# Router work inside an output projection, another order of weight buffers, and a sum of experts in two parts

## The chip, the core and the metric

The kernel runs on one core of a Trainium2 chip. Its time is the device time of one execution in microseconds (us). The engines in the rows are PE (TensorE, matrix products and transposes), PEld (its weight loads), DVE (VectorE), ACT (ScalarE), POOL (GpSimd) and SP (SyncE, which here issues most of the DMA transfers). An engine's instructions run in the order of its own queue; between engines they wait on semaphores.

## The reference

Two transformer blocks run one after the other on 256 tokens of 1024 features, in float32. The change lies in the first: a hybrid mixer ends in an output projection `w_out`, and behind it comes a mixture of 32 experts.

```python
x = x + gate_m * hybrid_mixer(...)            # ends in: merged @ w_out
h = rmsnorm(x, norm_ffn) * (1.0 + scale_f) + shift_f
x = x + gate_f * hierarchical_moe(h, ...)

def hierarchical_moe(h, w_rg, b_rg, w_re, b_re, w_gate, w_up, w_down):
    g_logits = tok @ w_rg + b_rg              # 4 groups; one is chosen
    e_logits = tok @ w_re + b_re              # 8 experts a group; two are chosen
    ...
    for e in range(N_EXPERTS):
        hid = silu(tok @ w_gate[e]) * (tok @ w_up[e])
        out = out + combine[:, e:e + 1] * (hid @ w_down[e])
```

The three weights of an expert are 1 MB each.

## The kernel before

**Dense products.** The activations lie with features on the partitions: `xT[:, n]` is a slice of 128 features by 256 tokens, and there are eight of them. `dense_B` makes each slice of an output as a tile: for each of eight slices k of the input three products (`mm3`, L653 to L655), since weights and input are both split into a high and a low part. With `lead=True` the first three tiles run interleaved by k, in the order in which the input slices become ready (`gate_of`); the others follow one by one, 24 products each. When a tile is done, `evac` is called: for the output projection, "wout", that is `ev_wout`, which adds the tile to `xT` (L1183), scales it for the router into `xa` (L1184) and hands it to `Squares`, whose ScalarE squares serve the mean of squares of the next norm.

**Weights.** The class `Weights` issues all loads on SyncE in one fixed order, each as soon as its buffer is free; a load whose buffer isn't free holds up all behind it. For dense layers a loaded piece becomes a unit: ScalarE copies its high part (L211), VectorE subtracts for the low one (L212), into slots called `whl`.

**Experts.** There are 96 expert matrices (eight groups of four experts, each gate, up, down), loaded as jobs 0 to 95 into 16 buffers in turn: nine `rawb`, two "w" (the `whl` slots 2 and 3, each taken as two halves), five `rawa`. The "w" buffers are handed to the loader by `ws.pool("w", ...)` only when wout and its units are done, in the code just ahead of the expert rounds. There are four rounds r, each with `gate_up(r, 0)`, `down(r, 0)`, `gate_up(r, 1)`, `down(r, 1)`; each product of the first kind is L1407. A round's result is put into `xT` by `combine` within the next round, after its first `gate_up`; the last one, `combine(*before, True)`, stands behind all rounds and makes the squares and sums for the final norm on the way. In round 1 a branch (`If`) leads to a slower path that is not taken with these inputs.

**Router.** The token-major copy of `xa` (transposes, L1203) and the 36 logits (L1204) are made slice by slice after wout. The norm's root (`rsqrt`, 12 small VectorE operations) and the bias row `rbb` turn them into `lg` (L1208); then come the choice of group and experts (L1239 to L1267), the tables of slots, and the products that gather the tokens (L1366), which feed the first `gate_up`. `token_major` makes the token-major activations `ht` from the transposes with help of ScalarE and GpSimd (L1221, L1222, L1229). The constant vector `b1` of the norm's shift is spread over tokens (`brow`) and run through the router weights by `shift_rows` (L1164 on): a generator put into `pipes`, of which `dense_B` runs a step at given places, four products, four, and eight.

**PSUM** has eight banks. `psum_banks(n)` gives n to the tag "acc" (tiles of `dense_B`) and 7 − n to "mis"; during wout n is 3.

Of the kernel before, what the change touches and what calls it, by code (L numbers as in the profile page):

```python
# [19 lines left out]
T = 256  # L20
# [249 lines left out]
def _trace(ctx, tc, A, out, dbg, stop):  # L270
# [9 lines left out]

    def psum_banks(n, **kw):

        pscope.close()
        psums["acc"] = n, pscope.enter_context(tc.tile_pool(name=f"pacc{n}", bufs=n, space=PSUM, **kw))
        psums["mis"] = 7 - n, pscope.enter_context(tc.tile_pool(name=f"pm{n}", bufs=7 - n, space=PSUM, **kw))

# [6 lines left out]
    def mis():  # L293
        return acc("mis")
# [52 lines left out]
    for pr in range(8):  # L347
        for m in ("expert_w_gate", "expert_w_up", "expert_w_down"):
            for e in range(4 * pr, 4 * pr + 4):
                src = A[m][0, e]  # L350
                q = j % (NA + NB + NW)
                pool = "b" if q < NB else "w" if q < NB + NW else "a"
                j += 1
                at = [(o, 1024) for o in (0, 1024)] if pool == "w" else [(0, 2048)]
                ws.add((m, e), [(None, bass.AP(tensor=src.tensor, offset=src.offset + o, ap=[[2048, 128], [1, n]]))
                                for o, n in at], (2048,), pool=pool)
# [206 lines left out]
    def run(g):  # L563
        for _ in g:
            pass
# [582 lines left out]
    with ExitStack() as l1:  # L1148
# [9 lines left out]
        gate = mods[0][:, 40:48]  # L1158
        xa = wk.tile([128, 8, T], FT, name="xa", tag="X", bufs=2)
        brow = wk.tile([128, 1024], FT, name="brow", tag="X", bufs=2)  # L1160
# [17 lines left out]

        pipes.append(shift_rows())
        sq = Squares()  # L1180

        def ev_wout(n, ps, w):
            V.scalar_tensor_tensor(xT[:, n], ps[:, :T], mods[0][:, 16 + n:17 + n], xT[:, n], op0=OP.mult, op1=OP.add)  # L1183
            V.tensor_scalar(xa[:, n], xT[:, n], a1[:, n:n + 1], None, op0=OP.mult)  # L1184
            sq.add(xT[:, n])

        dense_B("wout", cols256(0, 1024), 1024, lambda k: ohi[:, k], lambda k: olo[:, k], ev_wout, lead=True,
# [5 lines left out]
        if stop == "x_mix0":  # L1193
            return
        psum_banks(4, reuse_waits="tile")
        tp = [[acc() for _ in range(2)] for _ in range(2)]
        lps = [mis() for _ in range(2)]
        for kt in range(8):
            if kt == 3:
                ps = mis()  # L1200
                sq.mean(ps)
            for c in range(2):
                P.transpose(tp[kt // 4][c][:, kt % 4 * 128:kt % 4 * 128 + 128], xa[:, kt, c * 128:(c + 1) * 128], ident)  # L1203
                P.matmul(lps[c][:, :36], xa[:, kt, c * 128:(c + 1) * 128], wr[:, kt], start=(kt == 0), stop=(kt == 7))  # L1204
        rm = rsqrt(ps[:, 0:2])
        lg = wk.tile([128, 2, 36], FT, name="lg")
        for c in range(2):
            V.scalar_tensor_tensor(lg[:, c], lps[c][:, :36], rm[:, c:c + 1], rbb, op0=OP.mult, op1=OP.add)  # L1208

        hth = hl.tile([128, 2, 8, 128], FR, name="hth", tag="h8", bufs=2)  # L1210
        htl = hl.tile([128, 2, 8, 128], FR, name="htl", tag="h8", bufs=2)

        ht = wk.tile([128, 4, 512], FT, name="ht", tag="X", bufs=2)

        def token_major(g, c, eng):
            t_ = ht[:, 2 * g + c]
            bg = brow[:, g * 512:(g + 1) * 512]
            if eng is V:
                V.scalar_tensor_tensor(t_, tp[g][c], rm[:, c:c + 1], bg, op0=OP.mult, op1=OP.add)
            else:  # L1220
                S.activation(t_, tp[g][c], AF.Copy, scale=rm[:, c:c + 1])  # L1221
                G.tensor_tensor(t_, t_, bg, op=OP.add)  # L1222
            pv = t_.rearrange("t (a q k) -> t a q k", a=4, q=16)
            oh = hth[:, c].rearrange("t k (a q) -> t a q k", q=16)[:, 4 * g:4 * g + 4]
            ol = htl[:, c].rearrange("t k (a q) -> t a q k", q=16)[:, 4 * g:4 * g + 4]
            yield True
            S.activation(oh, pv, AF.Copy)
            yield True
            eng.tensor_tensor(ol, pv, oh.bitcast(FT), op=OP.subtract)  # L1229
# [221 lines left out]

        def combine(Ys, C, last=False):

# [4 lines left out]
            for f in range(8):  # L1458
                ps = mis()
                for p_ in range(2):  # L1460
                    for i in range(2):
                        P.matmul(ps[:, :T], Ys[p_][i][:, f * 128:(f + 1) * 128], C[p_][0], start=(p_ + i == 0),
                                 stop=(p_ + i == 2))
                V.scalar_tensor_tensor(xT[:, f], ps[:, :T], gate[:, f:f + 1], xT[:, f], op0=OP.mult, op1=OP.add)
# [12 lines left out]

        ws.pool("w", ws.whl, 2, 3)
        ws.pump()
        ready, before = deque(), None  # L1480
# [4 lines left out]
        for r in range(4):  # L1485
# [13 lines left out]
            next(nxt, None)  # L1499
            Ys = [down(r, 0, hT, C[0][1])]  # L1500
            hid = gate_up(r, 1, X)
            next(nxt, None)
# [6 lines left out]
            before = Ys, C  # L1509
        sums = combine(*before, True)  # L1510
        if stop == "moe":
# [653 lines left out]
```

## Time and profile before

| what | us |
|---|---|
| three runs | 1554.55, 1557.94, 1560.27 (median 1557.94) |
| the profiled execution, its own time | 1556.02 |
| its span | 1554.2 |
| busy: PE, DVE, ACT, POOL | 1380.5, 898.1, 633.0, 359.2 |
| wout, from its first product | 263.18 to 290.87 |
| wait for the first product of the router's gather (L1366) | until 311.31 |
| expert rounds, first to last product | 317.42 to about 537 |

All times within the kernel are from the start of the span of the profiled execution. The rows further below have their start first, then their length. A product's length in the rows (0.28 us for a dense one) is more than its share of the engine, since products overlap; the pace is read from the starts.

### The profile page before, as it was taken

What the parts mean: (1) busy time and instruction counts of PE and PEld (TensorE: products, weight loads), DVE (VectorE), ACT (ScalarE), POOL (GpSimd) and SP (SyncE); (2) the same over time, 40 slices, a digit from 0 to 9 for tenths busy, and PEclk for the clock granted to TensorE, in tenths of its full rate; (3) what the DMA queues carried; (4) which work ended last, traced back from release to release, by engine and by line L of the source; (5) the groups of instructions that cost most, each with busy time, mean ns of one, the idle gap of its engine ahead of it and who ended that gap; (6) DMA issues with size and microseconds to landing.
All of it is one profiled execution on the core that took longest, in us unless ns stands there. A gap on an engine that the chain in (4) does not pass through costs nothing.

```text
span 1554.2 us, 29404 instructions
## 1 busy us (share of the span) xinstructions
PE 1380.5 (89%) x12145; PEld 1184.7 (76%) x12145; DVE 898.1 (58%) x1683; ACT 633.0 (41%) x1117; POOL 359.2 (23%) x402
## 2 busy tenths in 40 slices
PE   3978699796687689999998899999999998999997
PEld 1757578763343389888997786899998887899997
DVE  3676666631112287877664566665555787765544
ACT  2633223320101257544443454454443766554432
POOL 3163642100000011154256203900000574000000
PEclk9998789896978889999999899999999999999998
DMA  8883456979999985655799976776557564877540
GB/s 309 295 284 125 154 163 217 361 293 418 374 417 419 359 140 152 209 180 170 178 179 168 234 200 204 208 207 178 174 182 217 177 190 136 244 193 188 176 150 28
DMA packets 283613, 344.00 MB, mean 221 GB/s; under 512 B 18249, under 2 KB 258368, under 8 KB 265552
## 3 DMA queue, kind: packets, MB, share of 16 engines
q1 hardware_dynamic: 272016, 335.33, 67.9%
q0 software_dynamic: 10848, 5.33, 3.5%
q8 instruction: 97, 1.59, 0.4%
q10 hardware_dynamic: 608, 1.39, 0.2%
q14 instruction: 44, 0.36, 0.1%
HBM read 340.63 MB, written 1.10 MB: 220 GB/s over the span
## 4 chain that ended last, share of the span: by engine, by line
PE 51%; DMA 9%; DVE 7%; ACT 3%; POOL 2%; issue 2%; POOLq 0%; SPq 0%; DVEq 0%; ACTq 0%
PE acc L653 14%; PE acc L654 14%; PE acc L655 14%; DMA rawa<-in_hy_w_in_dram 3%; DMA rawb<-in_expert_w_up_dram 3%; DVE wlo L212 2%; PE adaps L524 2%; POOL c L2029 1%; PE acc L1407 1%; DMA rawb<-in_expert_w_gate_dram 1%; PE mis L1740 1%; DMA rawa<-in_expert_w_up_dram 1%; DMA rawa<-in_expert_w_gate_dram 1%; ACT whi L211 1%; DVE q L1695 1%
## 5 line engine op out<-in xcount | busy, mean ns | idle before, releaser
L212 DVE TENSOR_TENSOR wlo<-rawa,whi 128x1024 fp32r<-128x1024 f32 (+1 forms) x303 | 378.2, 1252 | 252.2 <-ACT whi L211 251.4
L653 PE MATMUL acc<-hhi,whi 128*128 128x256 f32 (+2 forms) x1728 | 513.7, 297 | 9.4 <-ACT hhi L643 5.4
L654 PE MATMUL acc<-hlo,whi 128*128 128x256 f32 (+2 forms) x1728 | 500.0, 289 | 1.6 <-DVE hlo L649 1.2
L655 PE MATMUL acc<-hhi,wlo 128*128 128x256 f32 (+2 forms) x1728 | 498.1, 288 | 0.1
L653 PEld LDWEIGHTS acc<-hhi,whi 128*128 128x128 f32 (+2 forms) x1728 | 338.6, 196 | 45.1 <-issue 24.0
L211 ACT ACTIVATE whi<-rawa 128x1024 fp32r<-128x1024 f32 (+1 forms) x304 | 313.5, 1035 | 145.1 <-PE acc L654 105.2
L654 PEld LDWEIGHTS acc<-hlo,whi 128*128 128x128 f32 (+2 forms) x1728 | 338.9, 196 | 5.0 <-DVE hlo L649 4.2
L655 PEld LDWEIGHTS acc<-hhi,wlo 128*128 128x128 f32 (+2 forms) x1728 | 339.3, 196 | 0.5 <-DVE wlo L212 0.3
L653 PE MATMUL acc<-ghi,whi 128*128 128x256 f32 x352 | 99.6, 283 | 0.0
L654 PE MATMUL acc<-glo,whi 128*128 128x256 f32 x352 | 99.6, 283 | 0.0
L655 PE MATMUL acc<-ghi,wlo 128*128 128x256 f32 x352 | 99.6, 283 | 0.0
L1407 PE MATMUL acc<-rawb,X 128*32 128x256 f32 x576 | 63.9, 459 | 18.7 <-DMA rawb<-in_expert_w_gate_dram 10.9
L524 PE MATMUL adaps<-rawa,cs 128*32 128x512 f32 (+1 forms) x576 | 69.9, 587 | 6.0 <-DMA rawa<-in_w_ada_dram 6.0
L1979 POOL TENSOR_SCALAR dg<-cst,pcols 128x128 f32<-128x128 f32 x75 | 53.1, 726 | 84.1 <-PE acc L655 84.1
L1415 DVE TENSOR_TENSOR sq<-sq,acc 128x256 f32<-128x256 f32 x8 | 3.4, 421 | 117.0 <-PE acc L1407 117.0
L653 PEld LDWEIGHTS acc<-ghi,whi 128*128 128x128 f32 x352 | 67.6, 192 | 0.0
L654 PEld LDWEIGHTS acc<-glo,whi 128*128 128x128 f32 x352 | 67.6, 192 | 0.0
L655 PEld LDWEIGHTS acc<-ghi,wlo 128*128 128x128 f32 x352 | 67.6, 192 | 0.0
L1407 PE MATMUL acc<-rawa,X 128*32 128x256 f32 x320 | 45.4, 514 | 20.5 <-DMA rawa<-in_expert_w_up_dram 9.9
L1407 PEld LDWEIGHTS acc<-rawb,X 128*32 128x32 f32 x576 | 28.3, 131 | 43.3 <-DMA rawb<-in_expert_w_gate_dram 16.0
L1471 POOL TENSOR_TENSOR X<-X 128x256 f32<-128x256 f32 x5 | 3.9, 782 | 235.9 <-ACT X L1468 235.6
L1793 POOL DMA_DIRECT2D bt<-rbd x64 | 50.8, 806 | 31.7 <-DMA bt<-rbd 30.2
(598 smaller groups left out, 2415.0 us busy)
## 6 DMA issues: line engine op xcount, KB each, us to landing
rawa<-in_ada_w_dram SPq DMA_DIRECT2D x48, 1024.0 KB, 5.1
rawa<-in_w_ada_dram SPq DMA_DIRECT2D x24, 1024.0 KB, 8.2
rawa<-in_ffn_w_gate_dram SPq DMA_DIRECT2D x44, 512.0 KB, 4.0
rawa<-in_ffn_w_up_dram SPq DMA_DIRECT2D x44, 512.0 KB, 5.3
rawa<-in_hy_w_in_dram SPq DMA_DIRECT2D x20, 1024.0 KB, 7.4
rawa<-in_hy_w_in_dram SPq DMA_DIRECT2D x40, 512.0 KB, 7.5
rawb<-in_expert_w_gate_dram SPq DMA_DIRECT2D x18, 1024.0 KB, 19.9
rawb<-in_expert_w_up_dram SPq DMA_DIRECT2D x18, 1024.0 KB, 16.2
```

Source lines behind the costliest of these rows:

```text
L211: self.nc.scalar.activation(hv, src, AF.Copy)
L212: (engine or self.nc.vector).tensor_tensor(lv, src, hv.bitcast(FT), op=OP.subtract)
L524: P.matmul(ps[32 * g:32 * g + 32, :], cs[:, col + k:col + k + 1].to_broadcast([128, 32]), raw[:, k, g * w:(g + 1) * w], start=(q + k == 0) ...
L653: P.matmul(ps, wh, xh, start=start, stop=False)
L654: P.matmul(ps, wh, xl, start=False, stop=False)
L655: P.matmul(ps, wl, xh, start=False, stop=stop)
L1407: P.matmul(ps[32 * i:32 * i + 32, :256], X[:, kt, o:o + 32], half(raws[i], kt // 4)[:, kt % 4 * 256:kt % 4 * 256 + 256], start=(kt == 0), ...
L1695: V.scalar_tensor_tensor(a_[:, s_:], ps[:, :T - s_], cw[:, i:i + 1], a_[:, s_:], op0=OP.mult, op1=OP.add)
L1740: P.matmul(sg_[:, o:o + 128], Lm[:, c, a], Ub, start=True, stop=True)
L1793: nc.gpsimd.dma_start(bt[:, a, o + 64 * g:o + 64 * g + 64], bass.AP(tensor=rbd.tensor, offset=base + 511 + 127 * g, ap=[[0, 2], [1, 64], [ ...
L1979: G.tensor_scalar(diag[n][:, i], ident, tap(i, n), None, op0=OP.mult)
L2029: G.tensor_tensor(c2, c2, pr_, op=OP.add)
```

## The change

1. `psum_banks` can set aside a bank "log" for logits; during wout the split is 3 acc, 3 mis, 1 log.
2. `shift_rows` is run whole ahead of wout (`run(...)`) and is no longer a pipe within it.
3. A new function `route(kt)` makes the two transposes and the two logit products of a slice. `ev_wout(n)` calls it for slice n − 1; slice 7 follows behind the mean of squares. `xa` is now a buffer for one slice, two in turn. After slices 3 and 7 ScalarE copies the transposes into `ht`, and `token_major` works on `ht` in place.
4. Of the 16 expert buffers the two "w" ones come last, not tenth and eleventh; they are handed over right behind wout.
5. `combine` takes a list of the parts to sum. In round 3 the first four experts' part is added ahead of the second `gate_up`; the last `combine` adds the other four.

```diff
-                pool = "b" if q < NB else "w" if q < NB + NW else "a"
+                pool = "b" if q < NB else "a" if q < NB + NA else "w"
...
-        xa = wk.tile([128, 8, T], FT, name="xa", tag="X", bufs=2)
+        psum_banks(3, 1, reuse_waits="tile")
...
-        pipes.append(shift_rows())
+        run(shift_rows())
         sq = Squares()
+
+        ht = wk.tile([128, 4, 512], FT, name="ht", tag="X", bufs=2)
+        lpb = acc("log")
+        lps = [lpb[:, 64 * c:64 * c + 36] for c in range(2)]
+        tp, xas = [], []
+
+        def route(kt):
+
+            xa = xas.pop()
+            if kt % 4 == 0:
+                tp[:] = mis(), mis()
+            for c in range(2):
+                P.transpose(tp[c][:, kt % 4 * 128:kt % 4 * 128 + 128], xa[:, c * 128:(c + 1) * 128], ident)
+                P.matmul(lps[c][:, :36], xa[:, c * 128:(c + 1) * 128], wr[:, kt], start=(kt + c == 0), stop=(kt + c == 8))
+            if kt % 4 == 3:
+                for c in range(2):
+                    S.activation(ht[:, 2 * (kt // 4) + c], tp[c], AF.Copy)
 
         def ev_wout(n, ps, w):
             V.scalar_tensor_tensor(xT[:, n], ps[:, :T], mods[0][:, 16 + n:17 + n], xT[:, n], op0=OP.mult, op1=OP.add)
-            V.tensor_scalar(xa[:, n], xT[:, n], a1[:, n:n + 1], None, op0=OP.mult)
+            xa = wk.tile([128, T], FT, name="xa", tag="xa", bufs=2)
+            V.tensor_scalar(xa, xT[:, n], a1[:, n:n + 1], None, op0=OP.mult)
             sq.add(xT[:, n])
+            if n:
+                route(n - 1)
+            xas.append(xa)
...
-        psum_banks(4, reuse_waits="tile")
-        tp = [[acc() for _ in range(2)] for _ in range(2)]
-        lps = [mis() for _ in range(2)]
-        for kt in range(8):
-            if kt == 3:
-                ps = mis()
-                sq.mean(ps)
-            for c in range(2):
-                P.transpose(tp[kt // 4][c][:, kt % 4 * 128:kt % 4 * 128 + 128], xa[:, kt, c * 128:(c + 1) * 128], ident)
-                P.matmul(lps[c][:, :36], xa[:, kt, c * 128:(c + 1) * 128], wr[:, kt], start=(kt == 0), stop=(kt == 7))
+        ws.pool("w", ws.whl, 2, 3)
+        ws.pump()
+        ps = acc()
+        sq.mean(ps)
+        route(7)
...
+        psum_banks(4, reuse_waits="tile")
...
-                V.scalar_tensor_tensor(t_, tp[g][c], rm[:, c:c + 1], bg, op0=OP.mult, op1=OP.add)
+                V.scalar_tensor_tensor(t_, t_, rm[:, c:c + 1], bg, op0=OP.mult, op1=OP.add)
             else:
-                S.activation(t_, tp[g][c], AF.Copy, scale=rm[:, c:c + 1])
+                S.activation(t_, t_, AF.Copy, scale=rm[:, c:c + 1])
...
-        def combine(Ys, C, last=False):
+        def combine(Ys, C, last=False, fours=(0, 1)):
...
-                for p_ in range(2):
+                for p_ in fours:
...
-        ws.pool("w", ws.whl, 2, 3)
-        ws.pump()
...
             Ys = [down(r, 0, hT, C[0][1])]
+            if r == 3:
+                combine(Ys, C, fours=(0,))
...
-        sums = combine(*before, True)
+        sums = combine(*before, True, (1,))
```

Three places in the programs' order. In these rows `mis`, `acc` and `log` are PSUM tiles, `ohi` and `olo` the parts of wout's input, `mod` the modulations, `whi` and `wlo` the parts of a weight unit; line numbers of the kernel after are one higher up to wout.

TensorE at the start of wout, before:

```order
L543 MATMUL mis<-cst,adasb 128x128 [waits DVE_49,Activation_49]
L543 MATMUL mis<-cst,adasb 128x128 x3
L653 MATMUL acc<-ohi,whi_2540 128x256 [waits DVE_49,Activation_49]
L654 MATMUL acc<-olo,whi_2540 128x256 [waits DVE_49]
L655 MATMUL acc<-ohi,wlo_2541 128x256
```

and now:

```order
L544 MATMUL mis<-cst,adasb 128x128 [waits DVE_49,Activation_49]
L544 MATMUL mis<-cst,adasb 128x128 x3
L1171 MATMUL mis<-cst,mod_144 128x128 [waits DVE_49]
L1171 MATMUL mis<-cst,mod_144 128x128 x7
L1177 MATMUL mis<-wr,mod_144 128x36 [waits DMASW3_49,DMASW2_49,DVE_49]
L1177 MATMUL mis<-wr,mod_144 128x36 x7
L654 MATMUL acc<-ohi,whi_2540 128x256 [waits Activation_49]
L655 MATMUL acc<-olo,whi_2540 128x256
```

The sixteen products of `shift_rows` have moved from the inside of wout to a place ahead of its first product, and their first one waits for VectorE.

TensorE at the end of the three interleaved tiles, before:

```order
L653 MATMUL acc<-ohi,whi_2631 128x256
L654 MATMUL acc<-olo,whi_2631 128x256
L655 MATMUL acc<-ohi,wlo_2632 128x256
L653 MATMUL acc<-ohi,whi_2773 128x256 [waits DVE_49,Activation_49]
L654 MATMUL acc<-olo,whi_2773 128x256
```

and now:

```order
L656 MATMUL acc<-ohi,wlo_2632 128x256
L1194 MATMUL mis<-cst,xa 128x128 [waits DVE_49,Activation_49]
L1195 MATMUL log<-wr,xa 128x36
L1194 MATMUL mis<-cst,xa 128x128 [waits Activation_49]
L1195 MATMUL log<-wr,xa 128x36
L1194 MATMUL mis<-cst,xa 128x128 [waits DVE_49]
L1195 MATMUL log<-wr,xa 128x36
L1194 MATMUL mis<-cst,xa 128x128
L1195 MATMUL log<-wr,xa 128x36
L654 MATMUL acc<-ohi,whi_2807 128x256 [waits Activation_49]
```

Slices 0 and 1 of the router now stand between the interleaved tiles and the fourth tile, and each waits for VectorE, which writes `xa`.

SyncE's loads of the first expert matrices, before:

```order
L183 DMA rawb<-in_expert_w_down_dram 128x2048
L175 DMA whi_3130<-in_expert_w_down_dram 128x1024
L175 DMA wlo_3131<-in_expert_w_down_dram 128x1024
L175 DMA whi_3134<-in_expert_w_down_dram 128x1024
L175 DMA wlo_3135<-in_expert_w_down_dram 128x1024
L183 DMA rawa<-in_expert_w_down_dram 128x2048
L183 DMA rawa<-in_expert_w_gate_dram 128x2048 x4
L183 DMA rawb<-in_expert_w_up_dram 128x2048 x4
```

and now:

```order
L183 DMA rawb<-in_expert_w_down_dram 128x2048
L183 DMA rawa<-in_expert_w_down_dram 128x2048 x3
L183 DMA rawa<-in_expert_w_gate_dram 128x2048 x2
L175 DMA whi_3058<-in_expert_w_gate_dram 128x1024
L175 DMA wlo_3059<-in_expert_w_gate_dram 128x1024
L175 DMA whi_3062<-in_expert_w_gate_dram 128x1024
L175 DMA wlo_3063<-in_expert_w_gate_dram 128x1024
L183 DMA rawb<-in_expert_w_up_dram 128x2048 x4
```

The four halves into "w" buffers have moved behind the five `rawa` loads; the next load, the first into a buffer already used, is the same in both.

## Rows read from the trace of the kernel before

**Rows 1.** Windows: us, PE (instructions) PEld DVE ACT POOL, PEclk, DMA share, GB/s.

```profile
285.00:290.00 5.00, 5.00 (x44) 5.00 (x43) 2.34 (x6) 0.83 (x2) 0.00 (x0) 1.00 0.64 267
290.00:295.00 5.00, 5.00 (x51) 5.00 (x50) 1.96 (x8) 0.42 (x1) 0.00 (x0) 1.00 0.62 164
310.00:315.00 5.00, 3.69 (x17) 3.72 (x18) 1.43 (x8) 0.60 (x1) 0.00 (x0) 0.50 0.23 97
...
325.00:330.00 5.00, 3.30 (x27) 3.07 (x26) 2.90 (x13) 0.98 (x2) 0.00 (x0) 1.00 1.02 429
```

**Rows 2.** Timeline of SyncE's issues, 286 to 325: start, length, what.

```profile
293.53 2.01 SPq L183 DMA_DIRECT2D rawa<-in_expert_w_gate_dram  x4
321.09 1.99 SPq L183 DMA_DIRECT2D rawb<-in_expert_w_up_dram  x4
```

**Rows 3.** Chain of waits, 480 to 546: start, length, engine or transfer.

```profile
505.12 15.12 DMA rawa<-in_expert_w_up_dram
...
540.44 0.56 DVE X L1470
```

**Rows 4.** Timelines of PE and DVE at the start of wout.

```profile
262.60 0.63 PE L543 MATMUL mis<-cst,adasb 128*128 128x128 f32 x4
...
264.12 0.39 PE L654 MATMUL acc<-olo,whi 128*128 128x256 f32 x1 [0.56 <-DVE olo L1137]
...
263.65 2.77 DVE L1137 TENSOR_TENSOR olo<-oT,ohi 128x256 fp32r<-128x256 f32 x8
266.33 0.16 DVE L504 TENSOR_TENSOR mod<-mis,pcols 128x2 f32<-128x2 f32 x1
```

**Rows 5.** Timeline of PE within wout: the shift rows and what follows.

```profile
274.36 1.05 PE L1170 MATMUL mis<-cst,mod 128*128 128x128 f32 x8
275.17 0.36 PE L653 MATMUL acc<-ohi,whi 128*128 128x256 f32 x1
...
279.01 1.87 PE L1176 MATMUL mis<-wr,mod 128*128 128x36 f32 x16
280.71 0.36 PE L653 MATMUL acc<-ohi,whi 128*128 128x256 f32 x1
```

**Rows 6.** Timelines of PE and DVE: fourth tile, end of the interleaved ones.

```profile
272.85 0.36 PE L653 MATMUL acc<-ohi,whi 128*128 128x256 f32 x1
...
273.19 1.23 DVE L212 TENSOR_TENSOR wlo<-rawa,whi 128x1024 fp32r<-128x1024 f32 x1
...
274.85 0.35 DVE L1184 TENSOR_SCALAR xa<-xT,modA 128x256 f32<-128x256 f32 x1
```

**Rows 7.** Timelines of PE, DVE and POOL behind wout.

```profile
290.87 0.27 PE L1203 MATMUL acc<-cst,xa 128*128 128x128 f32 x1
...
291.41 0.30 PE L1203 MATMUL acc<-cst,xa 128*128 128x128 f32 x1
...
294.07 0.16 DVE L606 TENSOR_SCALAR nw<-mis 128x2 f32<-128x2 f32 x1 [1.79 <-PE mis L598]
...
296.04 0.16 DVE L611 SCALAR_TENSOR_TENSOR nw<-nw 128x2 f32<-128x2 f32 x1
...
298.24 0.22 DVE L1239 TENSOR_REDUCE v<-lg 128x8 f32<-128x64 f32 x1
...
298.75 1.30 DVE L1243 TENSOR_TENSOR o<-o,cst 128x64 f32<-128x64 f32 x1
...
304.89 0.22 DVE L1243 TENSOR_TENSOR o<-o,cst 128x64 f32<-128x64 f32 x1
...
298.72 2.49 POOL L1222 TENSOR_TENSOR ht<-ht,brow 128x512 f32<-128x512 f32 x2 [45.75 <-ACT ht L1221]
```

**Rows 8.** Windows at the clock's changes (columns as in rows 1), and PE's restart.

```profile
295.50:296.00 0.50, 0.50 (x6) 0.50 (x6) 0.43 (x3) 0.00 (x0) 0.00 (x0) 0.65 1.09 385
...
316.00:316.50 0.50, 0.50 (x5) 0.50 (x5) 0.00 (x0) 0.00 (x0) 0.00 (x0) 0.87 0.00 0
...
311.31 0.55 PE L1366 MATMUL mis<-adasb,hth 128*128 128x256 f32 x1 [2.70 <-DVE adasb L1355]
```

More of the change, by code (lines that the diff above doesn't have):

```diff
@@ L279, in _trace, with psum_banks @@
     psums, pscope = {}, ctx.enter_context(ExitStack())
-    def psum_banks(n, **kw):
+    def psum_banks(n, log=0, **kw):
         pscope.close()
-        psums["acc"] = n, pscope.enter_context(tc.tile_pool(name=f"pacc{n}", bufs=n, space=PSUM, **kw))
-        psums["mis"] = 7 - n, pscope.enter_context(tc.tile_pool(name=f"pm{n}", bufs=7 - n, space=PSUM, **kw))
+        for tag, k in (("acc", n), ("mis", 7 - n - log), ("log", log)):
+            if k:
+                psums[tag] = k, pscope.enter_context(tc.tile_pool(name=f"p{tag}{n}{log}", bufs=k, space=PSUM, **kw))
     psum_banks(3)
@@ L1208, in _trace @@
             V.scalar_tensor_tensor(lg[:, c], lps[c][:, :36], rm[:, c:c + 1], rbb, op0=OP.mult, op1=OP.add)
+        psum_banks(4, reuse_waits="tile")
         hth = hl.tile([128, 2, 8, 128], FR, name="hth", tag="h8", bufs=2)
         htl = hl.tile([128, 2, 8, 128], FR, name="htl", tag="h8", bufs=2)
-        ht = wk.tile([128, 4, 512], FT, name="ht", tag="X", bufs=2)
         def token_major(g, c, eng):
@@ L1459, in combine @@
                 ps = mis()
-                for p_ in range(2):
+                for p_ in fours:
                     for i in range(2):
-                        P.matmul(ps[:, :T], Ys[p_][i][:, f * 128:(f + 1) * 128], C[p_][0], start=(p_ + i == 0),
-                                 stop=(p_ + i == 2))
+                        P.matmul(ps[:, :T], Ys[p_][i][:, f * 128:(f + 1) * 128], C[p_][0],
+                                 start=(p_ == fours[0] and i == 0), stop=(p_ == fours[-1] and i == 1))
                 V.scalar_tensor_tensor(xT[:, f], ps[:, :T], gate[:, f:f + 1], xT[:, f], op0=OP.mult, op1=OP.add)
```

## The prediction

> **What bounds the kernel now.** I read the page first: by its first part TensorE is busy for most of the span, and the dense products lead the chain that ended last. That average hides stages with different limits, and the change lies in two of them.
>
> The first is the output projection ("wout", 263 to 291 us). The timeline of TensorE is gapless there; a dense product costs 0.12 us (twelve of them from 272.85 to 274.36) [rows 5, 6]. Whatever is put among them, or ahead of them, moves the end of the stage. Behind it comes a serial router: last tile, mean of squares, reciprocal root, logits, choice of group and experts, one-hot tables, first expert product (290.87 to about 317) [rows 7, 8].
>
> The second is the stream of expert weights. I read the windows from 285 to 330 next [rows 1]: DMA is at 0.62 to 0.64 of its capacity at the end of wout, at 0.23 from 310 to 315, and at 1.02 (429 GB/s) from 325 on. The list of SyncE's issues gives the reason: nothing is issued between 293.53 + 2.01 = 295.54 and 321.09, where the first load that reuses a buffer goes out [rows 2]. All sixteen buffers are full and wait for the first gate-and-up product. From there the stream is at its limit, and the chain of waits names transfers for most of the last round of experts (15.12 us for one piece) [rows 3]. So what delays the first expert product delays the restart of the loads, and a stream at its limit has no room to catch up: the delay arrives at the end. That is the frame of my sum: shift of the restart, plus what the last combine gives.
>
> **Part 1, the shift rows go ahead of wout.** These 16 products (a broadcast copy of the shift vector through TensorE, and the shift's part of the logits) stood inside wout. They now stand ahead of its first product on TensorE, and the first of them waits for the vector of modulations, which VectorE writes behind eight subtractions. Before, only the second product of wout waited, for the first of those eight (0.56 us), and ran at 264.12; the rest of the eight went on beside TensorE [rows 4]. The modulation is written at 266.33 + 0.16 = 266.49. The shift rows' own cost is read from the jumps that they make between dense products: 275.17 − 274.36 = 0.81, a second such piece, 0.80, and 280.71 − 279.01 = 1.70, so 3.31 us [rows 5]. New: 266.49 + 3.31 = 269.80 for the first product of wout, 269.92 for the second, against 264.12: +5.8. What was inside goes away: −3.3. Net **+2.5**, all of it idle TensorE. Queued behind the waiting product are all products of wout; VectorE and ScalarE go on with halves of weights that nobody takes yet, so nothing is won there.
>
> **Part 2, the router runs inside wout.** One slice of 128 features (two transposes, two products for 36 logits) takes 291.41 − 290.87 = 0.54 us in a row of such slices [rows 7]; with the handover to and from dense products I take 0.57. Slices 0 and 1 stand right behind the three interleaved tiles, and the fourth tile stands behind them. Slice 1 needs the second tile's scaled output, which VectorE writes at 274.85 + 0.35 = 275.20, because a 1.23 us subtraction for weights stands between the first tile's and the second's [rows 6]. So the fourth tile starts at 275.20 + 0.57 = 275.77 in place of 272.85: **+2.9** (bounds: 2 × 0.57 = 1.1 if that subtraction were done earlier in the longer idle time, 2.9 if it stays in place; its place in VectorE's row does not change, so 2.9). Slices 2 to 5 stand between later tiles, at operands long ready: 4 × 0.57 = **+2.3**. Slice 6 falls into the time in which TensorE waits for the last squares anyway: nothing; without that cover it is 0.57. End of wout so far: 2.5 + 2.9 + 2.3 = +7.7.
>
> **Part 3, what is saved behind wout.** Before, the logits waited for the last of 32 products, not for the root; the first reduction of the choice started at 298.24, which is 7.37 us after 290.87 [rows 7]. Now the last squares, the mean and the root set it: the mean's result is read at 294.07, 3.2 after the end of wout; the root ends at 296.04 + 0.16, 2.1 later; two logits, operations of the size of the 0.22 us ones, about 0.6 with their gaps: 5.9 in all. **−1.5**, of which I take −1.4. Bounds: 0, if GpSimd's four operations set the pace (the first two from 298.72), and −2.1, if they come so early that the slow VectorE operations beside them are fewer. For a small VectorE operation with two inputs took 1.30 us there, and one of the same line and shape 0.22 when GpSimd was done [rows 7]. The Trainium skill ("SBUF — State Buffer", "Who interferes with whom") calls this pair of ports a lock, held for a whole instruction; the trace agrees (1.30 against 0.22). By it the gain would be that of the whole block moving, the 1.4 that I have.
>
> **Part 4, the clock of TensorE.** This is the term that no row of wout shows, since its clock is 1.00 throughout. The nearest rows are at the router: it fell to its lower level (1.2 GHz, half) within 295.50 to 296.00, 4.7 us after the last dense product, with TensorE busy on small router products in all of that slice [rows 8]. So small products did not hold it. It came back within 316.00 to 316.50, 4.7 us after the dense-shaped products of 311.31 began [rows 8]. The change makes the same pattern at 263: TensorE's row of work ends at 262.60 + 0.63 = 263.2 [rows 4], then 3.3 us idle, then 3.3 us of shift rows, then dense products. By these rows the clock falls at 263.2 + 4.7 = 267.9: of the shift rows (266.5 to 269.8) 1.9 us run at half speed, +1.9; the dense products then start at 271.7, and 4.7 us at half speed lose 2.35. Sum **+4.3**. Bounds: 0 if it does not fall, 3.3 + 2.35 = 5.7 if it falls within the idle time. I take 4.3, since it is worked from the nearest fall. The Trainium skill ("TensorE: Matmul & The Clock Gate", "HAM oscillation — how this bites in real kernels") ties the fall to idle gaps between bursts; the trace does not agree that idleness is needed (busy 0.50 of 0.50 in the slice of the fall). By the page alone the term would be 0 here if the shift rows count as a burst; that is the first rival.
>
> **Part 5, the order of buffers.** Of the sixteen buffers the two that are made free only behind wout are now the last of the round, not the tenth and eleventh. Five loads that stood behind them on SyncE go out earlier, so the 3.7 us of DMA capacity that lie idle between 285 and 295 (5 × 0.36 + 5 × 0.38) get filled [rows 1]. Cost or gain: 0, because all sixteen buffers are full before 315 either way, and their reuse starts with the first expert product. What hides it is SyncE's pause from 295.54 to 321.09; if that cover went, it would be worth 3.7.
>
> **Part 6, the last sum in two parts.** The sum of the first four experts of the last round moves ahead of the last gate-and-up, where TensorE waits for weights (the 15.12 us piece) [rows 3]: free there. The last combine keeps two products a slice, in place of four. But the chain there names VectorE for every slice (0.56 us for one of its two operations) [rows 3], not TensorE, whose two products fewer are 0.24. So only the start, before VectorE has its first slice, is won, with its weight loads and handover: **−0.5** (bounds 0, and −1.9 if TensorE set the pace: 8 × 0.24).
>
> **Sum.** 7.7 − 1.4 + 4.3 − 0.5 = +10.1. The profiled execution took 1556.02, so 1566.1 like for like; it lies 1.9 below the median of the runs shown, so I state 1568.
>
> **Rivals.** (a) *The clock holds.* The shift rows count as work, or 3.3 us of idling are too few. For it: TensorE is never idle for long there; against it: the fall at 295.5 came on a busy engine. 7.7 − 1.4 − 0.5 = +5.8: 1563.7, which is within 0.5% (a measurement of this kernel can tell about that, 7.8 us). (b) *The clock is hit twice*: the wait of 2.9 us behind the interleaved tiles, with slices 0 and 1 around it, adds to the first; another 2 to 3 us of dense products at half speed, +12 to +13: 1571. (c) *Not slower.* The restart of the loads is not what counts, but the bytes moved from 264 on; then the filled 3.7 us are a gain, and the delay of wout is hidden under transfers: −3.7 − 0.5 = −4.2, 1553.7. It decides if any load is still under way when the first expert product ends; against it stand the windows, DMA at 0.23 from 310 to 315 with all buffers full [rows 1]. (d) *It does not do what it says*: the router products are held back to the end of wout by their waits; then part 1 and the clock alone are left, +2.5 + 4.3 − 0.5 = +6.3, 1564.2, within 0.5%.
>
> **How the numbers follow.** Forecast 0.45, (a) 0.25, (b) 0.12, (c) 0.10, (d) 0.08. The likeliest gives 1568. The range from 1557 to 1575 leaves out most of (c) and the far end of (b); its low end takes (a) with the lower bounds of parts 2 and 3 (5.8 − 1.8 − 0.7 = +3.3, 1561) less the 3 to 4 us by which single runs differ, its high end the upper bounds of parts 3 and 4 with (b). Slower by over 0.5%: nine tenths of the forecast (0.41), (b), and a fifth of (a), 0.58; within 0.5%: the rest of these, (d) and the near half of (c), 0.36; faster 0.06, the far half of (c), whose price is the least sure.
>
> **What would show it.** TensorE idle from 263.2 to about 266.5, then shift rows, with the first wout product near 270 to 272: part 1. A granted clock of 0.5 in windows of that stretch: part 4; 1.00 throughout: rival (a). The fourth tile waiting for the scaled output behind a weight subtraction: part 2. The first reduction of the choice 5.9 us after wout ends, not 7.4: part 3. SyncE's first reuse of a buffer later than 321 by the sum of these, and the end of the expert stream later by the same: the frame. If the stream ends later by less, or the shift in wout is under 5 us, the forecast is wrong.

## The result, and the profile after

The changed kernel took 1570.6 us (median of 8 runs, 1565.71 to 1572.26) against 1558.2 before (median of 8): a ratio of 1.007, 95% interval 1.005 to 1.009. It is slower by 12.4 us; forecast were 10.1, with 1568 as the time and 1557 to 1575 as the range. The profiled execution has a span of 1570.5.

One thing must be known to read the two traces side by side. The four transposes that stand ahead of wout start at 262.60 in the trace of before and at 266.92 in that of after, though nothing ahead of them was changed. In the experiments that also leave everything ahead untouched they start anywhere from 263.58 to 266.44: single executions differ by some us in the first stage, and that of before is the earliest here, that of after the latest. So every shift below is counted from these transposes, in each trace.

Start of wout after, timelines of TensorE and VectorE (start, length, engine, line and operation, idle time before it and what ended it), which answer to [rows 4]:

```profile
266.92 0.63 PE L544 MATMUL mis<-cst,adasb 128*128 128x128 f32 x4
270.86 3.78 PE L1171 MATMUL mis<-cst,mod 128*128 128x128 f32 x16 [3.31 <-DVE mod L505]
274.44 3.47 PE L1177 MATMUL mis<-wr,mod 128*128 128x36 f32 x16
277.71 0.56 PE L654 MATMUL acc<-ohi,whi 128*128 128x256 f32 x1
278.07 0.41 PE L655 MATMUL acc<-olo,whi 128*128 128x256 f32 x1
...
267.97 2.77 DVE L1138 TENSOR_TENSOR olo<-oT,ohi 128x256 fp32r<-128x256 f32 x8
270.65 0.16 DVE L505 TENSOR_TENSOR mod<-mis,pcols 128x2 f32<-128x2 f32 x1
```

TensorE idles for 3.31 us, until VectorE's L505 behind the eight subtractions. The shift rows then take 277.71 − 270.86 = 6.85 us, not the 3.31 that they took within wout [rows 5]. The windows over that stretch say why (us, PE, PEld, DVE, ACT, POOL, PEclk, DMA share, GB/s):

```profile
266.00:268.00 2.00, 1.55 (x14) 1.31 (x13) 0.94 (x5) 1.25 (x5) 0.00 (x0) 1.00 0.03 8
268.00:270.00 2.00, 0.00 (x0) 0.00 (x0) 2.00 (x8) 1.58 (x6) 0.00 (x0) 0.96 0.44 82
270.00:272.00 2.00, 1.14 (x5) 1.14 (x6) 0.96 (x6) 0.00 (x0) 0.00 (x0) 0.50 0.95 397
...
280.00:282.00 2.00, 2.00 (x11) 2.00 (x11) 0.00 (x0) 0.00 (x0) 0.00 (x0) 0.50 0.99 418
282.00:284.00 2.00, 2.00 (x13) 2.00 (x13) 0.00 (x0) 0.00 (x0) 0.00 (x0) 0.62 1.04 434
284.00:286.00 2.00, 2.00 (x19) 2.00 (x19) 0.00 (x0) 0.00 (x0) 0.00 (x0) 1.00 0.99 410
```

The granted clock fell to its lower level (1.2 GHz, half) in the last us of the idle time and came back near 283.5 (a fall in the middle of 268 to 270 would read 0.75, so 0.96 puts it near 269.8): 13.7 us at half speed, over all of the shift rows and the first 5.8 us of dense products.

The end of the interleaved tiles and the router after, TensorE, VectorE and SyncE, which answer to [rows 2, 6, 7]:

```profile
289.46 0.30 PE L1194 MATMUL mis<-cst,xa 128*128 128x128 f32 x1 [0.34 <-ACT whi L211]
...
291.48 0.33 PE L1194 MATMUL mis<-cst,xa 128*128 128x128 f32 x1 [1.28 <-DVE xa L1203]
...
292.07 0.36 PE L654 MATMUL acc<-ohi,whi 128*128 128x256 f32 x1
...
308.99 0.27 PE L1194 MATMUL mis<-cst,xa 128*128 128x128 f32 x1
...
291.07 0.35 DVE L1203 TENSOR_SCALAR xa<-xT,modA 128x256 f32<-128x256 f32 x1
...
314.68 0.22 DVE L1255 TENSOR_REDUCE v<-lg 128x8 f32<-128x64 f32 x1
...
336.93 2.10 SPq L183 DMA_DIRECT2D rawb<-in_expert_w_up_dram  x4
```

The fourth tile starts 3.1 us after the last interleaved product (288.84 + 0.12 = 288.96), where it started 0.1 after it before. The choice's first reduction comes 5.69 us after the end of wout, not 7.37. The first reuse of a buffer comes at 336.93.

### The profile page after: what moved, and what is told of

It reads as the page before. It is cut to its first block, busy times and chain, and to the rows that moved or that the text cites. A ratio compares the mean times of both kernels' runs of the same rounds, so it can differ in the third digit from the quotient of the medians.

```text
span 1570.5 us, 29421 instructions
## 1 busy us (share of the span) xinstructions
PE 1383.9 (88%) x12145; PEld 1186.7 (76%) x12145; DVE 901.9 (57%) x1691; ACT 635.3 (40%) x1121; POOL 359.2 (23%) x402
## 4 chain that ended last, share of the span: by engine, by line
PE 60%; DMA 18%; DVE 13%; ACT 4%; POOL 3%; issue 2%; SPq 0%; ACTq 0%; POOLq 0%; DVEq 0%
PE acc L654 15%; PE acc L655 15%; PE acc L656 15%; DMA rawa<-in_expert_w_up_dram 4%; DVE wlo L212 3%; DMA rawb<-in_expert_w_down_dram 3%; PE adaps L525 3%; DMA rawa<-in_expert_w_gate_dram 3%; DMA bt<-rbd 2%; DMA rawb<-in_expert_w_up_dram 2%; DMA rawa<-in_hy_w_in_dram 2%; DVE X L977 1%; PE acc L1423 1%; POOL c L2045 1%; ACT whi L211 1%
## 5 line engine op out<-in xcount | busy, mean ns | idle before, releaser
L212 DVE TENSOR_TENSOR wlo<-rawa,whi 128x1024 fp32r<-128x1024 f32 (+1 forms) x303 | 382.2, 1265 | 258.3 <-ACT whi L211 257.6
```

The costliest lines, as they stand in the source:

```text
L212: (engine or self.nc.vector).tensor_tensor(lv, src, hv.bitcast(FT), op=OP.subtract)
```

## The experiments

In the table all but the last two columns are from the traces. "Reuse" is the time from the four transposes to SyncE's first load into a used buffer (58.49 before: 321.09 − 262.60), "stream" the end of the last product with a gate or up weight (263.01 after the transposes before), and "next stage" the start of the 100th dense product of the stage that follows the experts (302.50 after them); all as differences to before. The timed columns are medians of runs, and the ratio to the runs of before on the same chip with its interval.

| kernel | transposes at | reuse | stream | next stage | median | ratio |
|---|---|---|---|---|---|---|
| after | 266.92 | +11.5 | +11.1 | +13.3 | 1570.6 | 1.007 [1.005, 1.009] |
| e1 shift rows back as a pipe | 265.07 | +3.1 | +2.6 | +4.7 | 1564.33 | 1.0037 [1.0019, 1.0055] |
| e2 before, shift rows first | 265.98 | +1.0 | +1.2 | +0.8 | 1558.97 | 1.0003 [0.9988, 1.0018] |
| e3 dense products in the wait | 265.59 | +7.3 | +7.1 | +9.0 | 1565.4 | 1.0048 [1.0033, 1.0064] |
| e4 before, 10 us delay | 263.61 | +10.4 | +10.8 | +10.4 | 1567.66 | 1.0069 [1.005, 1.0088] |
| e12 PSUM split later | 263.58 | +7.2 | +7.0 | +9.2 | 1566.39 | 1.0066 [1.0042, 1.0089] |
| e5 modulations first | 263.68 | +3.5 | +3.2 | +5.1 | 1561.16 | 1.0031 [1.0016, 1.0046] |
| e6 idle time only | 264.33 | +7.3 | +7.0 | +9.1 | 1566.73 | 1.0059 [1.0039, 1.0079] |
| e11 pipe, router a tile later | 266.44 | +1.0 | +0.6 | +2.7 | 1562.31 | 1.0031 [1.0016, 1.0045] |
| e7 last sum alone | 265.41 | 0.0 | +0.1 | +2.1 | 1559.82 | 1.0013 [0.9995, 1.0031] |
| e8 buffers alone | 264.52 | 0.0 | −0.5 | +1.7 | 1559.28 | 1.0009 [0.9991, 1.0027] |
| e9 both orders mended | 265.16 | +1.8 | +2.2 | +4.1 | 1559.78 | 1.0012 [0.9997, 1.0028] |

**e1: the shift rows back inside wout.**

```diff
 # after
-        run(shift_rows())
+        pipes.append(shift_rows())
```

> The kernel after, with the shift rows put back as a pipe within wout; all else of the change stays. Theory (the shift rows ahead of wout cost the idle wait and the fallen clock): the wait of 3.3 us and the half-speed stretch of 270 to 283 us go away, the granted clock is 1.00 from 262 to the end of wout, and the time is the kernel before plus what the rest costs: routes 0 and 1 with the wait for the scaled slice 3.0, routes 2 to 5 2.1, less 1.7 behind wout, so +3.4, about 1561.6 us. Rival (the cost sits in the router's place and the buffers): still +9 or more, 1567.

The reuse is 8.4 us earlier than in the kernel after (+3.1 for +3.4 forecast), with the clock at 1.00 up to the end of wout. So some three quarters of the loss hang on the place of the shift rows. What is left stands at the end of the interleaved tiles, TensorE waiting for the two scaled slices:

```profile
275.70 0.30 PE L1194 MATMUL mis<-cst,xa 128*128 128x128 f32 x1 [0.34 <-DVE xa L1203]
277.72 0.33 PE L1194 MATMUL mis<-cst,xa 128*128 128x128 f32 x1 [1.20 <-DVE xa L1203]
```

The timed median lies 6.5 above that of before, more than the trace's 3 at the reuse; some 2 of the rest are lost behind the stream (see e7 and e8).

**e2: that edit alone, on the kernel before.**

```diff
 # before
-        pipes.append(shift_rows())
+        run(shift_rows())
```

> The kernel before, with one edit alone: the shift rows run whole ahead of wout. Theory: TensorE idles 3.3 us for the modulations, the 16 products take 3.3 at full clock and about 6.8 at half, and the dense products behind them run at half speed for about 5.7 us; less the 3.3 that leave wout: +5.8 - 3.3 + 3.5 + 2.8 = +8.8, about 1567 us. Rival (the clock falls only with the router's products beside): full clock throughout, +2.5, 1560.7.

A miss: +8.8 expected, +1.0 in the trace, and the timed runs cannot tell it from before. The rows of TensorE:

```profile
265.98 0.63 PE L543 MATMUL mis<-cst,adasb 128*128 128x128 f32 x4
266.44 1.95 PE L1170 MATMUL mis<-cst,mod 128*128 128x128 f32 x16
269.91 1.97 PE L1176 MATMUL mis<-wr,mod 128*128 128x36 f32 x16 [1.52 <-DVE mod L504]
271.72 0.36 PE L653 MATMUL acc<-ohi,whi 128*128 128x256 f32 x1
```

The first eight shift products (16 in the row, which counts each twice) run right behind the transposes, without any wait, and they read all of the shift vector. So the vector was there. Only the third tile waits, 1.52 us, and again for VectorE's last operation on the modulations. The clock fell here too, for 3.4 us from 272.3 on, and wout ends 2.3 us later than before (30.52 behind the transposes, 28.27 before). Of this 1.3 come back behind wout, where the row of small products ran at a clock of 1.00 to its end at 302.6; before, the same row ran at half speed from 295.65 on.

The difference between e2 and after that bears on the wait is the split of PSUM: four banks for "mis" here, three there. That made a new theory: what the first shift product waits for in the kernel after is not the vector, but its PSUM bank, out of which that same VectorE operation has yet to read.

**e12: the new theory, tested by one line moved.**

```diff
 # after
-        psum_banks(3, 1, reuse_waits="tile")
...
         run(shift_rows())
+        psum_banks(3, 1, reuse_waits="tile")
```

> The kernel after, with one line moved: the split of PSUM into 3 acc, 3 mis and 1 log comes behind the shift rows, not ahead of them, so that they rotate over four mis banks as in e2. Theory (the first shift product waits for its PSUM bank, which VectorE empties with the operation behind the eight subtractions, and not for the modulations themselves): the first eight shift products start right behind the transposes without a wait, the third tile waits 1.5 us as in e2, wout's second product comes about 5.2 us earlier than in the kernel after, and the first reuse of a buffer, measured from the transposes ahead of wout, about 5 us later than before in place of 11.5; about 1563 us. Rival (it waits for the modulations as data): the 3.3 us wait stays, 1570.

The wait is that of e2, not that of after:

```profile
263.58 0.63 PE L544 MATMUL mis<-cst,adasb 128*128 128x128 f32 x4
264.05 1.95 PE L1170 MATMUL mis<-cst,mod 128*128 128x128 f32 x16
267.51 2.07 PE L1176 MATMUL mis<-wr,mod 128*128 128x36 f32 x16 [1.51 <-DVE mod L505]
```

Same data, same order, the old banks: the bank theory stands. The built programs name the banks. Ahead of the shift rows VectorE's L505 still has to read bank 4 and L546 bank 5, while 6 and 7 are free. In e2 and e12 the three shift tiles take 7, 6 and 4; in the kernel after, bank 7 is set aside for "log", and they take 4, 6 and 5. So it is not only that a bank is lost: the new split also begins with one that is still unread. Three banks that begin with 6 were not run. wout's second product comes 5.0 us earlier than in the kernel after (5.2 forecast). The reuse came to +7.2, not +5: the clock fell twice, near 269 and again behind the wait for the second scaled slice (windows 268 to 274 and 282 to 286):

```profile
268.00:270.00 2.00, 2.00 (x17) 2.00 (x17) 0.38 (x2) 0.15 (x1) 0.00 (x0) 0.81 0.99 414
270.00:272.00 2.00, 2.00 (x11) 2.00 (x11) 0.95 (x1) 0.00 (x0) 0.00 (x0) 0.50 1.03 430
272.00:274.00 2.00, 2.00 (x16) 2.00 (x15) 0.00 (x0) 0.00 (x0) 0.00 (x0) 0.83 1.01 426
...
282.00:284.00 2.00, 1.94 (x13) 1.95 (x14) 1.89 (x5) 1.45 (x3) 0.00 (x0) 0.73 0.99 410
284.00:286.00 2.00, 2.00 (x11) 2.00 (x10) 1.13 (x1) 0.04 (x1) 0.00 (x0) 0.50 1.05 430
```

**e5: VectorE's order mended.** Draining the pipes first puts VectorE's operations on the modulations ahead of the eight subtractions.

```diff
 # after
+    drain()
     pipes.append(halves())
     drain()
```

> The kernel after, with the pipes run to their end before the halving of wout's input is queued, so that VectorE's two operations on the modulations stand ahead of the eight subtractions. Both theories of the wait (bank or data) say that it shrinks from 3.3 to under 0.6 us. What it tells is the clock: shift rows of 3.3 us right behind the transposes, then dense products. If want of dense work of some 4.4 us lowers the clock: about 1.5 us lost as in e2, reuse about +3.7 against before, 1562. If idle time is needed: full clock to the end of the interleaved tiles, reuse about +2.2, 1560.

The wait is 0.62 us, and the clock holds:

```profile
264.93 2.05 PE L1172 MATMUL mis<-cst,mod 128*128 128x128 f32 x16 [0.62 <-DVE mod L505]
...
266.00:268.00 2.00, 2.00 (x21) 2.00 (x20) 1.71 (x6) 1.80 (x5) 0.00 (x0) 1.00 0.71 279
268.00:270.00 2.00, 2.00 (x19) 2.00 (x19) 1.27 (x2) 0.56 (x1) 0.00 (x0) 1.00 1.00 422
270.00:272.00 2.00, 2.00 (x19) 2.00 (x18) 0.05 (x1) 0.00 (x0) 0.00 (x0) 1.00 1.03 430
```

So 3.6 us of small products behind a short wait did not lower it in this execution; of the two expectations the one on idle time holds for the clock. The reuse is +3.5, though, for +2.2: the wait of 0.62 and the 3.59 us of shift rows move wout's second product by 3.5 us (268.72 is 5.04 behind the transposes, before it was 1.52), which uses up the 3.3 that left wout. Against the kernel after, 8 us come back by an order of two VectorE operations, with the shift rows where the change has put them.

**e6: the idle time alone.** The shift rows are a pipe, as in e1, but one small product waits ahead of wout as the first shift product does in the kernel after.

```diff
 # e1
+        ps = mis()
+        P.matmul(ps[:, 0:36], b1[:, 7:8].to_broadcast([128, 128]), wr[:, 7], start=True, stop=True)
         pipes.append(shift_rows())
```

> The kernel e1 (shift rows as a pipe within wout), with a single small product ahead of wout that waits as the first shift product of the kernel after does: the 3.3 us of idle time alone, without the 16 products behind. If idle time alone lowers the clock: it falls near 3 us into the gap as in the kernel after, and 1.5 to 2.9 us are lost on the first dense products; reuse +8 to +9 against before (e1's 3.05, the wait of 3.3, and the loss), 1566. If the small products are needed for it: full clock, reuse +6.5, 1564.5.

```profile
268.27 0.41 PE L1181 MATMUL mis<-wr,mod 128*128 128x36 f32 x2 [3.30 <-DVE mod L505]
...
268.00:270.00 2.00, 1.73 (x13) 1.73 (x14) 1.51 (x5) 0.00 (x0) 0.00 (x0) 0.94 0.99 410
270.00:272.00 2.00, 2.00 (x12) 2.00 (x11) 0.00 (x0) 0.00 (x0) 0.00 (x0) 0.50 1.03 430
272.00:274.00 2.00, 2.00 (x14) 2.00 (x14) 0.00 (x0) 0.00 (x0) 0.00 (x0) 0.71 0.99 418
```

The idle time, with one small product behind it, lowered the clock, though only after the dense products had begun again, and for 3.4 us (2 × 0.06 × 2, 2, and 2 × 0.29 × 2, from the three windows' shortfalls). It costs 1.4 us by the remainder (wout's end is 9.71 behind that of before: e1's 5.44, 2.87 at the second product, and 1.4). The stay of 13.7 us in the kernel after is four times as long; what it has more than e6 is the shift rows behind the idle time.

**e3: the wait filled.** 26 dense products on a weight unit that lies ready, their result unread, stand ahead of the shift rows.

```diff
 # after
+        uw = ws.unit(("wout", 0, 0, 0))[0]
+        ps = acc()
+        for i in range(26):
+            P.matmul(ps[:, :T].rearrange("p (a b) -> p a b", b=128), uw[:, i % 4, :], uw[:, 4:6, :], start=True, stop=True)
         run(shift_rows())
```

> The kernel after, with 26 products of the dense shape, whose result nobody reads, ahead of the shift rows: they fill the 3.3 us wait for the modulations (26 x 0.12 = 3.1) and add no dependence. Theory (the clock falls for want of dense work between 267 and 278): the last dense product is then near 270.5, the shift rows take 3.3 at full clock, and wout starts at full clock or loses little: 5 to 6 us less than the kernel after, about 1565. Rival (the clock falls by the small products themselves, or at a place that the wait does not set): 3 us of half speed stay on the dense products behind, 1567 to 1568; if nothing changes, 1570.6.

```profile
266.32 3.38 PE L1183 MATMUL acc<-whi 128*128 128x256 f32 x26
269.53 2.04 PE L1171 MATMUL mis<-cst,mod 128*128 128x128 f32 x16
271.42 1.87 PE L1177 MATMUL mis<-wr,mod 128*128 128x36 f32 x16
273.12 0.36 PE L654 MATMUL acc<-ohi,whi 128*128 128x256 f32 x1
```

The shift rows start no earlier (3.94 us behind the transposes, as in the kernel after), yet they take 273.12 − 269.53 = 3.59 in place of 6.85, and the reuse is 4.2 us earlier than in the kernel after. About 1.7 more is lost again, since the clock, which held here, fell behind the next wait, that for the second scaled slice, for 3.4 us:

```profile
284.00:285.00 1.00, 0.65 (x6) 0.65 (x7) 1.00 (x2) 1.00 (x2) 0.00 (x0) 0.91 1.02 426
285.00:286.00 1.00, 1.00 (x6) 1.00 (x6) 0.89 (x3) 0.45 (x2) 0.00 (x0) 0.50 1.03 426
```

That is the place of rival (b), seen here and in e12, but not in the kernel after.

**e4: a delay by itself.** 84 dense products, unread, between wout and the router of the kernel before.

```diff
 # before
+        ps = acc()
+        for i in range(84):
+            P.matmul(ps[:, :T], ohi[:, i % 4, 0:128], ohi[:, 5], start=True, stop=True)
         psum_banks(4, reuse_waits="tile")
```

> The kernel before, with 84 products of the dense shape, whose result nobody reads, between the last tile of wout and the router's products: a delay of 84 x 0.12 = 10.1 us at full clock and nothing else. Theory (what delays the first expert product delays the restart of the loads, and the stream carries it to the end): first reuse of a buffer 10.1 later than 321, the end of the expert stream 10 later, time +10, about 1568. Rival (the stream has room to catch up, for example at the branch in round 1 where it pauses): the stream's end moves by 6 or less, 1564.

Reuse +10.4, end of the stream +10.8, timed +9.8: the stream gives nothing back, neither at the branch in round 1 nor elsewhere. The frame of the prediction holds, and rival (c) falls. (The profiled execution is the shortest of the six, and the stretch behind its stream is 3.4 us shorter than before, 1025.2 for 1028.6, which is how single executions differ there.)

**e11 and e9: the router a tile later.** Slice n − 2 follows tile n, so that no slice waits for an output just made; slice 6 goes into the wait for the last squares. e11 is e1 with this, e9 is e5 with this.

```diff
-            xa = xas.pop()
+            xa = xas.pop(0)
...
         def ev_wout(n, ps, w):
             V.scalar_tensor_tensor(xT[:, n], ps[:, :T], mods[0][:, 16 + n:17 + n], xT[:, n], op0=OP.mult, op1=OP.add)
+            if n > 1:
+                route(n - 2)
             xa = wk.tile([128, T], FT, name="xa", tag="xa", bufs=2)
...
-            if n:
-                route(n - 1)
             xas.append(xa)
+            if n == 7:
+                route(6)
```

> The kernel e1 (shift rows as a pipe), with the router's slices one tile later: slice n - 2 behind tile n, slice 6 in the wait for the last squares. Theory (in e1 the 3.05 us left are the wait for the second scaled slice behind a weight subtraction and the four slices within wout, less the gain behind it): the fourth tile starts within 1 us of the end of the interleaved tiles, reuse +0.5 to +1 against before, 1558 to 1559, which cannot be told from before. Rival (the slices within wout cost by themselves, wherever they stand): +3 stays, 1561.

> The kernel after, with the two mended orders together: VectorE's operations on the modulations ahead of the eight subtractions (e5), and the router's slices one tile later (as in e11); the shift rows stay ahead of wout. Theory (the ledger of waits adds up): from e5's +3.5 at the first reuse of a buffer the lag takes 2.1 as it did from e1 to e11, so +1.4, full clock throughout; time 1558.5 to 1560. If a wait or the clock comes in at another place, +3 or more.

In both some 2 us came back: from +3.1 to +1.0 and from +3.5 to +1.8 at the reuse. Of the waits at the end of the interleaved tiles one is left, of 0.34 us in e11 and 0.25 in e9. At the reuse both are within 2 us of before; timed, e9 cannot be told from before, and e11 lies 5 above it. Neither beats the kernel before.

**e7 and e8: the other two parts alone.** The last sum in two parts (`combine` with `fours`, on the kernel before), and the order of the buffers (with the hand-over right behind wout, on the kernel before); each takes the change's own lines.

> The kernel before, with the last sum of experts in two parts alone. The prediction said -0.5 us (bounds 0 and -1.9). By the traces so far it is 0: from the last expert product to the final sums it takes 18.5 us in kernels with the change and 18.5 in e2 and e4 without it. So the time is that of before, 1557.5, within 2. Rival (the sum put ahead of the last gate-and-up delays it, since its VectorE operations run into it): 1 to 2 us more, and the last expert product comes later by that.

> The kernel before, with the order of the expert buffers alone (nine, five, two; the last two handed over right behind wout). The prediction said 0: the loads go out earlier ahead of the router, and the first reuse of a buffer stays at the first gate-and-up product, 58.5 us behind the transposes ahead of wout; the DMA share from 285 to 295 is 1.0 in place of 0.63. Rival (the order costs in the last round, where down weights now come last into the two slots, or in the stream): 1 to 3 us more at the last expert product.

Timed, neither can be told from before. In e7 the time from the last expert product to the final sums is the same to 0.01 us (525.61 to 543.75 before). In e8 the loads do go out earlier, and DMA has no idle share left there, against 0.64 and 0.62 in [rows 1]:

```profile
285.00:290.00 5.00, 5.00 (x44) 5.00 (x43) 1.72 (x5) 0.84 (x2) 0.00 (x0) 1.00 1.02 423
290.00:295.00 5.00, 5.00 (x48) 5.00 (x46) 2.34 (x6) 0.83 (x2) 0.00 (x0) 1.00 1.02 423
```

The reuse stays where it was (0.0), since it waits for the first expert product.

Behind the stream, though, both lose some 2 us. The final sums (L1475) and the first dense product of the next stage, before and then in e7:

```profile
543.75 2.56 PE L1475 MATMUL acc<-gf,X 128*128 128x2 f32 x16 [1.17 <-ACT X L1466]
551.32 0.58 PE L653 MATMUL acc<-hhi,whi 128*128 128x256 f32 x1 [0.51 <-ACT hhi L643]
...
546.66 3.54 PE L1475 MATMUL acc<-gf,X 128*128 128x2 f32 x16 [1.48 <-ACT X L1466]
555.21 0.58 PE L653 MATMUL acc<-hhi,whi 128*128 128x256 f32 x1 [0.51 <-ACT hhi L643]
```

Before, the clock came back within the last sum (1.00 from 542 to 544). In e7, whose last sum has two products a slice in place of four, it stayed at 0.50 from 541 to 561: the final sums take 3.54 us in place of 2.56, and the dense products behind start at half speed and stay there for 6.0 us, not 3.8. From the end of the stream to the 100th dense product of the next stage it takes 39.5 us before, 39.0 in e2 and 39.1 in e4, but 41.4 in e7, 41.7 in e8, and 41.4 to 41.7 in all eight kernels that have both parts. e8 has the full last sum. There the clock came back for the final sums (1.00 from 544 to 546), but the dense products ran at half speed for 6.4 us. The final sums take 3.54 or 3.55 us in eight of the nine kernels with the split (2.98 in e5) and 1.92 to 2.76 in the four without, so the slow last sum goes with the split. The slow dense products behind it do not need it, by e8; why the clock is low there is open. Further on, idle stretches of up to 2.8 us that the profile puts down to no engine differ between executions; at the 600th product 1.5 us are left on average (108.4 to 110.6 without either part, 110.7 to 111.2 with one or both).

## Why the prediction was right, step by step

**The frame** was right, by e4. In the kernel after the reuse came +11.5 later, the stream's end +11.1, the span's end +12.0. That the total came so near the forecast is in part luck, since the parts below err both ways.

**Part 1** had its size right: 3.31 us of idle time measured, where the sum had 266.49 − 263.23 = 3.3. Its reason was wrong. "The first of them waits for the vector of modulations" fails by e2 and e12: it waits for a PSUM bank, since the change took one of four from "mis" for the logits and began the three that are left with an unread one. The VectorE operation that empties the bank also writes modulations, though not the shift vector, so both reasons gave the same time: luck. They differ in what they advise: by mine the shift rows could not have gone ahead of wout without the wait; by the runs the old four banks halve it (1.51 us in e12).

**Part 2**: +2.9 forecast for the start of the fourth tile, 3.0 measured, through the weight subtraction between the two scaled slices as named; e1 shows the two waits, e11 and e9 that the longer one can be avoided. The four slices within wout: 0.53 each (one from 298.52 to 299.05), 2.1 for 2.3.

**Part 3**: 5.69 us from the end of wout to the choice for 5.9 forecast, a gain of 1.7 for 1.4. Up to the reuse the gain is 2.3 (30.22 us from the end of wout before, 27.94 after); 0.5 of it lies between the gather's first product and the first expert product (6.11 and 5.59).

**Part 4** is the term that was mis-sized: 4.3 forecast, bounds 0 and 5.7; measured 6.85 − 3.31 = 3.5 on the shift rows and 2.6 on the interleaved products (11.25 us from 277.71 to 288.96 for 72 × 0.12 = 8.6), 6.1 in all, past the upper bound. The clock fell 2.3 us after the transposes ended (267.55), not 4.7, so all of the shift rows ran at half speed; and it rose 5.8 us after the dense products began, not 4.7. At the end of wout the shift is 13.8 us (42.07 behind the transposes, 28.27 before) where the sum had 7.7 + 4.3 = 12.0, and this term is the difference. The forecast took its 4.7 us from a fall behind the last dense product on a busy engine, and counted them from the transposes. e5 against e6 speaks for idle time in their place: 3.30 us of it lowered the clock with a single small product behind them, and 3.6 us of small products behind 0.62 of idle time did not. The Trainium skill ("TensorE: Matmul & The Clock Gate", "HAM oscillation — how this bites in real kernels") ties the fall to idle gaps; for this place e5 and e6 agree (1.00 and 0.50 at 270 to 272), against what the prediction held of it. But the length of a gap does not decide by itself: gaps of 1.3 to 1.5 us stand ahead of the falls in e2, e3 and e12, and gaps of 1.2 to 1.35 us lowered nothing in e1, e5, e6 and after. The fall of [rows 8] on a busy engine is not explained by these runs either; in e2 the same row of small products ran at 1.00 to its end.

**Part 5**: 0, as forecast, up to the reuse (0.0 in e8); for the 2.2 us that e8 lost behind the stream the sum has no term. **Part 6**: −0.5 forecast, bounds 0 and −1.9. Up to the final sums 0.0 was measured (e7), but by the 100th product of the next stage 1.9 are lost (41.4 for 39.5), because the clock stayed at its lower level; the sum counted only the last sum itself.

**The rivals**: (a) did not happen in the kernel after, but in e5, where the wait was short. (b), a fall behind the interleaved tiles, was seen in e12 on top of a first one, and in e3 alone. (c) falls by e4. (d) falls by the trace: slices 2 to 5 stand between the tiles (slice 3 at 298.52).

**What stays open.** The clock fell behind the wait of about 1.3 us at the interleaved tiles in e3 and e12, and not in e1, e5, e6 or after. It is open, too, why the clock is low behind the stream in e8. The shifts at the 100th product of the next stage agree with the timed medians to 2.4 us in every kernel; the widest misses are e11 (+2.7 in the trace, +5.0 timed), e1 (+4.7 and +6.5) and e9 (+4.1 and +2.4). Runs of one kernel spread over some 2 to 13 us, and each trace is one run. That the clock falls within wout in some executions of e1 and e11 and not in the profiled one would explain these two, but no run shows it.

## What to carry to other kernels

A step that is moved ahead of a dense stage costs its waits first: look at which PSUM bank its first product takes and who has yet to read it, not only at its data. An idle gap of some 3 us ahead of small products cost twice here, since they then ran at half clock and so did the dense products behind; filling the gap, or moving two VectorE operations, was worth more here (4.2 and 8.0 us) than the 1.7 that the change gained behind wout. Ahead of a stage that waits for its first product, earlier loads bought nothing. And taking products out of a stage that VectorE sets won no time there (e7), while the stage behind it started at half clock for longer.

## What the runs showed of the hardware that was not expected

Dense products whose result nobody reads, put into an idle gap, made the kernel 4.2 us faster at the reuse (e3 against after; 5.2 by the timed medians): the granted clock stayed at 1.00 there. The stay at half speed was 3.4 us in each of the falls that dense products followed at once (e2, e3, e6, e12), but 13.7 us where the 16 small products came first (after). And the same row of small products behind wout, in the same order in both programs, ran at 1.00 to its end in e2 and at half speed from 295.65 on before: the clock at a place can differ where the work there is the same.
